# Third and fourth product exchanged in the later blocks of an input phase, with their row factors computed on VectorE

## The chip, the cores and the metric

The kernel runs on one core of a Trainium2 chip. A core has five engines with instruction queues of their own, which the profile names PE (TensorE: matmuls; PEld is its weight load), DVE (VectorE), ACT (ScalarE), POOL (GpSimd) and SP (SyncE, which here only issues DMAs). The queues run side by side and wait for each other by semaphores. Within a queue the instructions of this program run in the order in which they stand.

The metric is the device time of one execution in microseconds (us). The time before is the median of three executions, 921.17 us, with the lowest at 918.97 and the highest at 922.02.

## The reference

With a depth of 1 only the pooling mixer runs: a norm over rows, an input projection into `u` and `gate`, trailing means of `u` over windows of 2, 4, 8 and 16 frames for four groups of 256 channels, a linear map for each group, the product with `silu(gate)`, the output projection, the residual and a final norm. `x` has 4096 rows of 1024 float32 numbers.

```python
def rms_norm(x, w):
    y = xf * lax.rsqrt(jnp.mean(xf * xf, axis=-1, keepdims=True) + RMS_EPS)
    return (y * w.astype(jnp.float32)).astype(x.dtype)

def pool_mixer(h, in_w, group_w, group_b, scale, out_w):
    u, gate = jnp.split(h @ in_w, 2, axis=-1)
    ...
    pooled = jnp.stack([trailing_mean(ug[:, :, g], w) for g, w in enumerate(POOL_WINDOWS)],
                       axis=2) - ug
    mixed = jnp.einsum('bsgc,gcd->bsgd', pooled, group_w) + group_b
    y = mixed.reshape(b, s, POOL_WIDTH) * scale * jax.nn.silu(gate)
    return y @ out_w

h = x + pool_mixer(rms_norm(x, norm_w), ...)
return rms_norm(h, final_norm_w)
```

## The kernel before

**Seven products instead of eight.** Each matrix product is cut into 2 x 2 blocks and done with seven block products, P1 to P7, on sums and differences of the blocks (the Winograd form of Strassen's method). The kernel has 112 such products, which its list of steps (L949 to L951) puts one behind the other: phase "a" (half of the input projection) for four blocks of 1024 rows, phase "b" (the other half) for the same four blocks, and phase "o" (the output projection) for eight blocks of 512 rows. In the phases "a" and "b" the order within a block is `ORDER_IN`, P1, P2, P6, P7, P5, P4, P3. A block of rows has a half 0 ("11" and "12" are its two halves of the channels) and a half 1 ("21" and "22").

**Operands.** TensorE takes each operand as a high and a low part. `split` (L153) makes them: ScalarE copies the operand into the rounded format (the high part, L151), and VectorE subtracts that copy from the operand (the low part, L145). `mm3` (L565) then issues three matmuls for each pair: high with high, high with low, low with high. So the first matmul of a product uses high parts alone, and the second needs a low part. A product in the phases "a" and "b" is 48 matmuls of 128x512 into four of the eight PSUM banks. There are four operand buffers (`ops`), two for each product, so a product's split waits until the product two steps before it has read its buffers.

**Banks.** `bank_of` (L574): P1, P2, P7 and P4 use banks 0 to 3; P6, P5 and P3 use banks 4 to 7. P1 goes through its banks one after the other; the others go through all four with the first half of the depth and then through all four again with the second. `evict_in` (L699) reads the results. ScalarE copies P1's four banks into banks 4 to 7, where P6 and P5 go on adding; P2 is added to P1 in banks 0 to 3, and ScalarE takes the sum through SiLU into two tiles; ScalarE copies P6 into two tiles and P7 into two others; VectorE adds P5 to P7's tiles and P4 to P6's; ScalarE copies P3.

**Forming the operands of phase "a".** P1 takes "11" and P2 takes "12", multiplied by the row factors of half 0 (`normalize`, L454). P6 takes "22" - ("11" - "21") and P7 takes "11" - "21", with "21" and "22" multiplied by the row factors of half 1. `normalize_a2` (L526) does the four multiplications of half 1; it is called as the step of P1 begins (L1211), ahead of P2's split. The four differences (`form_in`, L507, for P6) come right behind it. `form_s4` (L548) takes P6's operand from "12", for P3. P5 takes "11" plus P6's operand. While an operand is split, ScalarE's queue issues a DMA that saves "11", "12", "21" (as P7's operand) and "22" for phase "b" (`split_halves`, L469).

**Row factors.** For block b+1 they are made while block b is multiplied. ScalarE squares and sums rows (`square_row`, L403); `stats` (L412) calls `rsqrt` (L190): ScalarE's square root, VectorE's reciprocal, and one Newton step, which for blocks 1 to 3 is POOL's: `ms` (L193), two products, a multiply-add and a last product (L206 to L211). At the next step `store_rs` (L419) writes the 512 factors to DRAM from POOL's queue, and `load_rstd` (L449) loads them back spread over all partitions, also from POOL's queue. Block 0 goes another way, by matmuls (`spread_rs`).

**Pooling.** `pool` (L617) runs some steps behind the products: VectorE forms the window sums, subtracts and multiplies by the SiLU tile, and SP stores that product to DRAM (`yd`, L685). Its tiles return to a rotation from which later evictions and loads take theirs (`Slots`, `take`); a tile that is taken again must first have been read by whatever used it, a store included.

**What sets the order.** The main loop (L1193 to L1257) walks through the steps. At step n it issues loads up to three steps ahead, the squares and `stats`, the forming of step n + 2 (ahead of the split, unless `normal` holds, L1213: then behind it), the split of step n + 1, due pooling, and the matmuls and evictions of step n. A scheduler then places the instructions on each engine; `tc.issue_after(x)` keeps what stands in it behind instruction x. With block 2 `save_t3` (L273) prepares a difference of weight blocks for phase "b", behind P6: for each of two halves two loads, a subtraction on VectorE and a store. During block 3 the weights of phase "b" are formed and split (`form_wb`, `split_wb`).

**The end.** Behind the last product stand 36 matmuls (L1259 to L1280) that multiply operands still in SBUF with one another in several layouts, into banks that nothing reads afterwards.

Of the kernel before, what the change touches and what calls it, by code (L numbers as in the profile page):

```python
# [15 lines left out]
P = 128  # L16
# [4 lines left out]
NB = S // TB  # L21
# [10 lines left out]
ORDER_IN = (P1, P2, P6, P7, P5, P4, P3)  # L32
ORDER_OUT = (P1, P7, P6, P2, P5, P4, P3)
# [27 lines left out]
def kernel(  # L61
# [128 lines left out]
    def rsqrt(dst, tmp, ms, ss, on_vector=False):  # L190

        root = nc.scalar.activation(tmp, ss, AF.Sqrt, bias=eps, scale=1.0 / D).ins
        nc.gpsimd.tensor_scalar(  # L193
# [218 lines left out]
    def stats(b, half):  # L412
# [3 lines left out]
        rsqrt(rs, tmp, ms, sums[b, half], b == 0)  # L416
# [79 lines left out]

    def load_in(q, b, i):
        s = xs[b]
        if i == P1:
            s["11"] = load_saved(b, P1) if q else load_x(b, 0, 0)  # L500
        elif i == P2:
            s["12"] = load_saved(b, P2) if q else load_x(b, 0, 1)
        elif i == P6:
            s["21"] = load_saved(b, P7) if q else load_x(b, 1, 0)
            s["22"] = load_saved(b, P4) if q else load_x(b, 1, 1)

    def form_in(q, b, i):  # L507

        s = xs[b]
        if i in (P1, P2):  # L510
            if q == 0:
                for u in s["11" if i == P1 else "12"]:
                    normalize(b, 0, u)
        elif i == P6:
            s["2"] = [take() for _ in range(2)]
            for h in range(2):
                if q == 0:
                    sub(s["21"][h], s["11"][h], s["21"][h])
                sub(s["2"][h], s["22"][h], s["21"][h])
        elif i == P5:  # L520
# [4 lines left out]

    def normalize_a2(b):  # L526
        for h in range(2):
            normalize(b, 1, xs[b]["21"][h])
            normalize(b, 1, xs[b]["22"][h])
        give(rstd.pop(b))  # L530

    def split_in(q, b, i):
# [8 lines left out]
        if i not in (P1, P2, P6):  # L541
# [407 lines left out]
    steps = [("a", b, i) for b in range(NB) for i in ORDER_IN]  # L949
# [230 lines left out]
    def row_plan(b):  # L1180
        if b == 0:
# [5 lines left out]
            {P1: (0, 1), P2: (2, 3), P6: (4, 5), P7: (6, 7)},  # L1187
            {P6: (0, 1), P7: (2, 3), P5: (4, 5), P4: (6, 7)},
# [4 lines left out]
    for n in range(2, len(steps)):  # L1193
        kind, b, i = steps[n]
        ahead = kind == "a" and b + 1 < NB
        keep[0] = 5 if kind == "b" and b == NB - 1 else 3
        advance("load", n, load, load_reach)
        if ahead:
# [5 lines left out]
            for j in squares.get(i, ()):  # L1204
                with tc.issue_after(evicted[0]):
                    square_row(b + 1, j // 4, j % 4)
                if j % 4 == 3:
                    scales[j // 4] = stats(b + 1, j // 4)
            for j in rows.get(i, ()):
                load_row(b + 1, j // 4, j % 4, early if b == 0 and i == P6 else None)  # L1210
        if kind == "a" and b > 0 and i == P1:  # L1211
            normalize_a2(b)
        normal = kind == "a" and step(n + 2)[2] in (P1, P2)  # L1213
# [3 lines left out]
        if normal:  # L1217
            with tc.issue_after(latest_split[0]):
                form(n + 2)
        if n == 2:  # L1220
# [37 lines left out]

    sets = sets_of("o", NBO - 1)  # L1259
    left, right = ops[0], w[P1][0]  # L1260
    ways = (
        lambda r: r[:, 0:256].rearrange("p (s a) -> p a s", s=2),
        lambda r: r.rearrange("p (s a) -> p a s", s=2)[:, 0:128],
        lambda r: r[:, 0:256],
        lambda r: r.rearrange("p (m s a) -> p m a s", m=2, s=2),
    )
# [66 lines left out]
```

## Time and profile before

| | us |
|---|---|
| median of three executions | 921.17 |
| lowest and highest | 918.97, 922.02 |
| the profiled execution | 921.6 |
| its span, first to last instruction | 919.8 |
| mean granted TensorE clock | 1.000 of full speed |

The page's second part cuts the span into 40 slices of 23 us. Each digit is the busy share of an engine in tenths.

```profile
PE   9999999999989999999999999999999999999999
PEld 7888888878878888888888888888888888888888
DVE  3898993795697997496686588589988677676675
ACT  6869447347345565346345545654424424324333
POOL 0023101001100000000000000000001001001010
```

Phase "a" fills the slices 3 to 14, phase "b" those to 27, phase "o" the rest. TensorE is at 9 nearly throughout, but a digit of 9 covers a hole of up to 2.3 us. In a line of the timeline stand the start, the duration from the first to the last of the merged instructions, engine, line, operation, output and inputs, form and count, and in brackets how long the engine was idle before and what ended that. A line of the waits gives who waited for whom, the total in us, the number of waits and the longest.

The work of the stages, by windows of the profile (each line: the stretch in us, its length, the busy time of PE, PEld, DVE, ACT and POOL with their instructions, the granted clock, the share and the rate of DMA). The four stretches are about one block of phase "a" each:

```profile
66.00:108.00 42.00, 42.00 (x196) 36.77 (x195) 38.14 (x46) 31.15 (x47) 13.15 (x14) 1.00 0.69 243
108.00:181.00 73.00, 72.22 (x335) 62.93 (x334) 52.66 (x56) 39.22 (x63) 5.18 (x14) 1.00 0.60 204
181.00:256.00 75.00, 73.24 (x340) 63.82 (x339) 55.69 (x59) 39.30 (x64) 5.09 (x14) 1.00 0.64 229
256.00:332.00 76.00, 73.38 (x339) 63.63 (x338) 69.80 (x75) 39.81 (x59) 0.00 (x0) 1.00 0.62 229
```

(The first of them begins inside block 0.)

### The profile page before, as it was taken

How to read it: one execution, taken by the hardware profiler on the slowest of the kernel's cores; microseconds unless marked ns; L12 is line 12 of the kernel's file. 1: busy time of each engine (PE TensorE's matmuls, PEld its weight loads, DVE VectorE, ACT ScalarE, POOL GpSimd, SP SyncE). 2: the span in 40 equal slices, each digit the busy share in tenths (PEclk: the TensorE clock that was granted, in tenths of full speed). 3: DMA queues.
4: the chain of work that ended last, by engine and by line, in shares of the span. 5: the costliest groups of instructions: out<-in, count | busy, mean ns of one | idle time of the engine just before them, and what ended most of it. 6: DMA issues, size and time to landing. Idle time of an engine off the chain costs nothing.

```text
span 919.8 us, 11280 instructions
## 1 busy us (share of the span) xinstructions
PE 910.0 (99%) x4248; PEld 793.3 (86%) x4248; DVE 702.7 (76%) x769; ACT 458.2 (50%) x741; POOL 51.6 (6%) x130
## 2 busy tenths in 40 slices
PE   9999999999989999999999999999999999999999
PEld 7888888878878888888888888888888888888888
DVE  3898993795697997496686588589988677676675
ACT  6869447347345565346345545654424424324333
POOL 0023101001100000000000000000001001001010
DMA  9986666565756626116604725746656446356122
GB/s 342 402 313 212 268 237 202 184 248 205 252 229 238 219 109 216 42 46 229 251 37 134 275 92 195 244 149 203 233 178 230 147 150 229 122 199 210 42 92 92
DMA packets 66518, 177.02 MB, mean 192 GB/s; under 512 B 6048, under 2 KB 23840, under 8 KB 66464
## 3 DMA queue, kind: packets, MB, share of 16 engines
q1 hardware_dynamic: 59888, 154.78, 47.4%
q10 hardware_dynamic: 4176, 13.65, 3.7%
q0 software_dynamic: 2400, 7.88, 2.5%
q8 instruction: 33, 0.54, 0.2%
q14 instruction: 21, 0.17, 0.1%
HBM read 115.45 MB, written 60.83 MB: 192 GB/s over the span
## 4 chain that ended last, share of the span: by engine, by line
PE 79%; DVE 9%; DMA 6%; ACT 4%; issue 2%; SPq 0%; POOL 0%; DVEq 0%; ACTq 0%; POOLq 0%
PE bank L570 78%; DMA early<-in_wut 2%; DVE st L148 2%; DVE op L145 2%; DMA st<-in_x 2%; DMA st<-rd 1%; DMA rd<-rs 1%; DVE vt L142 1%; DVE st L145 1%; ACT op L151 1%; ACT early L407 1%; DVE st L142 1%; ACT st L407 1%; ACT vt L407 1%; PE bank L1275 1%
## 5 line engine op out<-in xcount | busy, mean ns | idle before, releaser
L570 PE MATMUL bank<-op,w 128*128 128x512 f32 x2688 | 582.3, 379 | 6.4 <-DVE op L145 5.7
L570 PEld LDWEIGHTS bank<-op,w 128*128 128x128 f32 x2688 | 507.5, 189 | 80.6 <-DVE op L145 7.8
L570 PE MATMUL bank<-w,op 128*128 128x512 f32 (+1 forms) x1356 | 290.3, 377 | 0.0
L570 PEld LDWEIGHTS bank<-w,op 128*128 128x128 f32 x1356 | 254.6, 189 | 35.8
L151 ACT ACTIVATE op<-st 128x1024 fp32r<-128x1024 f32 x126 | 132.4, 1052 | 167.1 <-PE bank L570 150.3
L145 DVE TENSOR_TENSOR op<-st,op 128x1024 fp32r<-128x1024 f32 x126 | 152.9, 1221 | 69.7 <-ACT op L151 69.4
L151 ACT ACTIVATE op<-vt 128x1024 fp32r<-128x1024 f32 x40 | 42.2, 1056 | 76.4 <-PE bank L570 66.3
L151 ACT ACTIVATE vt<-bank 128x512 f32<-128x512 f32 x102 | 58.5, 593 | 37.0 <-PE bank L570 35.0
L913 DVE TENSOR_TENSOR st<-bank,st 128x512 f32<-128x512 f32 x60 | 41.0, 686 | 29.3 <-PE bank L570 29.1
L145 DVE TENSOR_TENSOR st<-st,st 128x1024 f32<-128x1024 f32 x38 | 46.0, 1222 | 20.6 <-DMA st<-wvd 9.2
L145 DVE TENSOR_TENSOR op<-vt,op 128x1024 fp32r<-128x1024 f32 x40 | 48.8, 1221 | 7.8 <-ACT op L151 7.6
L193 POOL TENSOR_SCALAR oms<-oss 128x2 f32<-128x2 f32 x14 | 9.2, 659 | 607.1 <-ACT st L802 601.0
L151 ACT ACTIVATE bank<-bank 128x512 f32<-128x512 f32 x48 | 27.9, 581 | 26.9 <-PE bank L570 21.5
L142 DVE TENSOR_TENSOR vt<-bank,vt 128x512 f32<-128x512 f32 (+1 forms) x55 | 35.9, 678 | 2.2 <-PE bank L570 2.2
L651 DVE TENSOR_TENSOR_SCAN vt<-vt,bf 128x512 f32<-128x512 f32 x28 | 34.5, 1269 | 0.2 <-ACT vt L151 0.2
L913 DVE TENSOR_TENSOR vt<-bank,vt 128x512 f32<-128x512 f32 (+1 forms) x37 | 24.8, 673 | 12.0 <-PE bank L570 11.7
L145 DVE TENSOR_TENSOR w<-st,w 128x1024 fp32r<-128x1024 f32 x20 | 24.2, 1220 | 12.3 <-ACT w L151 12.3
L673 DVE SCALAR_TENSOR_TENSOR vt<-vt,vt 128x1024 f32<-128x1024 f32 x24 | 29.1, 1214 | 0.0
L148 DVE TENSOR_TENSOR st<-st,st 128x1024 f32<-128x1024 f32 (+1 forms) x19 | 21.7, 1163 | 9.7 <-DMA st<-rd 9.0
L151 ACT ACTIVATE w<-st 128x1024 fp32r<-128x1024 f32 x20 | 20.9, 1055 | 16.2 <-PE bank L570 14.9
L806 DVE SCALAR_TENSOR_TENSOR st<-st,ors,st 128x1024 f32<-128x1024 f32 x17 | 21.4, 1281 | 6.1 <-POOL ors L211 6.1
L151 ACT ACTIVATE vt<-vt 128x1024 f32<-128x1024 f32 (+1 forms) x12 | 11.8, 985 | 25.2 <-DVE vt L142 21.6
(132 smaller groups left out, 570.9 us busy)
## 6 DMA issues: line engine op xcount, KB each, us to landing
st<-in_x SPq DMA_DIRECT2D x33, 512.0 KB, 5.1
st<-sd SPq DMA_DIRECT2D x29, 512.0 KB, 4.8
st<-in_xt SPq DMA_DIRECT2D x25, 512.0 KB, 6.7
vt<-in_x SPq DMA_DIRECT2D x24, 512.0 KB, 4.6
sd<-st ACTq DMA_DIRECT2D x19, 512.0 KB, 4.4
yd<-vt SPq DMA_DIRECT2D x19, 512.0 KB, 2.9
st<-yd SPq DMA_DIRECT2D x19, 512.0 KB, 4.4
out<-st SPq DMA_DIRECT2D x17, 512.0 KB, 4.2
```

The lines of the kernel that those rows point to most:

```text
L142: nc.vector.tensor_tensor(out=dst, in0=a, in1=b, op=ALU.add)
L145: return nc.vector.tensor_tensor(out=dst, in0=a, in1=b, op=ALU.subtract)
L148: nc.vector.tensor_tensor(out=dst, in0=a, in1=b, op=ALU.mult)
L151: return nc.scalar.activation(dst, src, func)
L193: nc.gpsimd.tensor_scalar(out=ms, in0=ss, scalar1=1.0 / D, scalar2=EPS, op0=ALU.mult, op1=ALU.add)
L407: nc.scalar.activation(u[:, 0], u[:, 0], AF.Square, accum_out=sums[b, half][:, j : j + 1])
L570: latest[0] = nc.tensor.matmul(ps, a, b, start=start and n == 0, stop=stop and n == 2, skip_group_check=True).ins
L651: nc.vector.tensor_tensor_scan(s[:, j, at:end], v[:, j, at:end], v[:, j, at - win : end - win], sums_of[j] if sums_of else 0.0, ALU.add, A ...
L673: nc.vector.scalar_tensor_tensor(out=s[:, :, at : at + H], in0=s[:, :, at : at + H], scalar=1.0 / win, in1=v[:, :, HIST:], op0=ALU.mult, o ...
L806: nc.vector.scalar_tensor_tensor(out=us[j], in0=us[j], scalar=rs[:, j : j + 1], in1=fw[0], op0=ALU.mult, op1=ALU.mult,)
L913: partial["added"] = nc.vector.tensor_tensor(out=dst, in0=src, in1=dst, op=ALU.add).ins
L1275: nc.tensor.matmul(ps.rearrange("p (m a s) -> p m a s", m=2, s=2) if c == 3 else ps.rearrange("p (a s) -> p a s", s=2) if c < 2 else ps, l ...
```

## The change

1. In the blocks 1, 2 and 3 of phase "a" the order becomes P1, P2, P7, P6, P5, P4, P3. "21" is loaded for P7 and "22" for P6, a step later than before.
2. `normalize_a2` is gone. For P7 the two multiplications of "21" and the differences "11" - "21" are formed together; for P6 those of "22" and the differences with P7's operand. For P7, P6 and P5 of those blocks forming comes behind the latest split, as it did for P1 and P2.
3. `stats` runs behind the latest split of its step instead of ahead of it, and for the blocks 1 to 3 all of its small operations but the square root are VectorE's. In block 0 `ms` stays on POOL.
4. The plan of the rows that are squared names P7 and P6 in exchanged places, so each row keeps its step.
5. `save_t3` still follows P6 of block 2, which is now the fourth step of the block.
6. The 36 matmuls at the end are left out.

The number of matmuls of the products, of wide operations and of loads and stores is the same.

```diff
--- before.py
+++ after.py
@@ -30,6 +30,7 @@
 
 P1, P2, P3, P4, P5, P6, P7 = range(1, 8)
 ORDER_IN = (P1, P2, P6, P7, P5, P4, P3)
+ORDER_LATER = (P1, P2, P7, P6, P5, P4, P3)
 ORDER_OUT = (P1, P7, P6, P2, P5, P4, P3)
 
 
@@ -190,7 +191,7 @@
     def rsqrt(dst, tmp, ms, ss, on_vector=False):
 
         root = nc.scalar.activation(tmp, ss, AF.Sqrt, bias=eps, scale=1.0 / D).ins
-        nc.gpsimd.tensor_scalar(
+        (nc.vector if on_vector == "all" else nc.gpsimd).tensor_scalar(
             out=ms, in0=ss, scalar1=1.0 / D, scalar2=EPS, op0=ALU.mult, op1=ALU.add
         )
         nc.vector.reciprocal(out=dst, in_=tmp)
@@ -413,7 +414,7 @@
         ms = small.tile([P, 4], F32, tag="ms", name=f"ms{b}_{half}")
         tmp = small.tile([P, 4], F32, tag="tmp", name=f"tmp{b}_{half}")
         rs = small.tile([P, 4], F32, tag="rs", name=f"rs{b}_{half}")
-        rsqrt(rs, tmp, ms, sums[b, half], b == 0)
+        rsqrt(rs, tmp, ms, sums[b, half], "all" if b else "most")
         return rs
 
     def store_rs(b, half, rs):
@@ -494,14 +495,20 @@
             us.append(u)
         return us
 
+    def swapped(q, b):
+        return q == 0 and b > 0
+
     def load_in(q, b, i):
         s = xs[b]
         if i == P1:
             s["11"] = load_saved(b, P1) if q else load_x(b, 0, 0)
         elif i == P2:
             s["12"] = load_saved(b, P2) if q else load_x(b, 0, 1)
+        elif i == P7 and swapped(q, b):
+            s["21"] = load_x(b, 1, 0)
         elif i == P6:
-            s["21"] = load_saved(b, P7) if q else load_x(b, 1, 0)
+            if not swapped(q, b):
+                s["21"] = load_saved(b, P7) if q else load_x(b, 1, 0)
             s["22"] = load_saved(b, P4) if q else load_x(b, 1, 1)
 
     def form_in(q, b, i):
@@ -511,23 +518,24 @@
             if q == 0:
                 for u in s["11" if i == P1 else "12"]:
                     normalize(b, 0, u)
+        elif i == P7 and swapped(q, b):
+            for h in range(2):
+                normalize(b, 1, s["21"][h])
+            for h in range(2):
+                sub(s["21"][h], s["11"][h], s["21"][h])
         elif i == P6:
             s["2"] = [take() for _ in range(2)]
             for h in range(2):
                 if q == 0:
-                    sub(s["21"][h], s["11"][h], s["21"][h])
+                    normalize(b, 1, s["22"][h])
                 sub(s["2"][h], s["22"][h], s["21"][h])
+            if q == 0:
+                give(rstd.pop(b))
         elif i == P5:
             for h in range(2):
                 add(s["11"][h], s["2"][h], s["11"][h])
             for u in s.pop("2"):
                 give(u)
-
-    def normalize_a2(b):
-        for h in range(2):
-            normalize(b, 1, xs[b]["21"][h])
-            normalize(b, 1, xs[b]["22"][h])
-        give(rstd.pop(b))
 
     def split_in(q, b, i):
         s = xs[b]
@@ -538,7 +546,10 @@
             stores.extend(zip(sd[0][i], s[key]))
         if i == P6 and (q or b):
             form_s4(b)
-        if i not in (P1, P2, P6):
+        if i == P6 and swapped(q, b):
+            for u in s.pop("21"):
+                give(u)
+        elif i not in (P1, P2, P6) and not (i == P7 and swapped(q, b)):
             for u in s.pop(key):
                 give(u)
         return t
@@ -946,7 +957,7 @@
 
 
 
-    steps = [("a", b, i) for b in range(NB) for i in ORDER_IN]
+    steps = [("a", b, i) for b in range(NB) for i in (ORDER_LATER if b else ORDER_IN)]
     steps += [("b", b, i) for b in range(NB) for i in ORDER_IN]
     steps += [("o", b, i) for b in range(NBO) for i in ORDER_OUT]
     split_up = {}
@@ -1184,8 +1195,8 @@
                 {P7: range(4), P5: (4, 5), P4: (6, 7)},
             )
         return (
-            {P1: (0, 1), P2: (2, 3), P6: (4, 5), P7: (6, 7)},
-            {P6: (0, 1), P7: (2, 3), P5: (4, 5), P4: (6, 7)},
+            {P1: (0, 1), P2: (2, 3), P7: (4, 5), P6: (6, 7)},
+            {P7: (0, 1), P6: (2, 3), P5: (4, 5), P4: (6, 7)},
         )
 
     scales = {}
@@ -1193,6 +1204,7 @@
     for n in range(2, len(steps)):
         kind, b, i = steps[n]
         ahead = kind == "a" and b + 1 < NB
+        rows_done = None
         keep[0] = 5 if kind == "b" and b == NB - 1 else 3
         advance("load", n, load, load_reach)
         if ahead:
@@ -1205,18 +1217,22 @@
                 with tc.issue_after(evicted[0]):
                     square_row(b + 1, j // 4, j % 4)
                 if j % 4 == 3:
-                    scales[j // 4] = stats(b + 1, j // 4)
+                    rows_done = j // 4
             for j in rows.get(i, ()):
                 load_row(b + 1, j // 4, j % 4, early if b == 0 and i == P6 else None)
-        if kind == "a" and b > 0 and i == P1:
-            normalize_a2(b)
-        normal = kind == "a" and step(n + 2)[2] in (P1, P2)
+        ahead_of = step(n + 2)
+        normal = kind == "a" and ahead_of[2] in (P1, P2) or (
+            ahead_of[0] == "a" and ahead_of[1] > 0 and ahead_of[2] in (P7, P6, P5)
+        )
         if n > 2 and not normal:
             form(n + 2)
         advance("split", n, split_step, split_reach)
         if normal:
             with tc.issue_after(latest_split[0]):
                 form(n + 2)
+        if rows_done is not None:
+            with tc.issue_after(latest_split[0]):
+                scales[rows_done] = stats(b + 1, rows_done)
         if n == 2:
             with tc.issue_after(first_saves[0]):
                 for place, u in stores:
@@ -1256,29 +1272,6 @@
                 )
                 fw.append(f)
 
-    sets = sets_of("o", NBO - 1)
-    left, right = ops[0], w[P1][0]
...
-    with tc.issue_after(latest[0]):
-        for c, way in enumerate(ways):
-            for j in range(9):
...
-                nc.tensor.matmul(
...
```

16 lines of the change are left out of this document (removed).

## The prediction

> **What bounds the kernel now.** I read the page first, then TensorE's waits, its timeline, and the timelines of VectorE and ScalarE around each hole.
>
> ```profile
> PE 910.0 (99%) x4248; PEld 793.3 (86%) x4248; DVE 702.7 (76%) x769; ACT 458.2 (50%) x741; POOL 51.6 (6%) x130
> ...
> L570 PE MATMUL bank<-op,w 128*128 128x512 f32 x2688 | 582.3, 379 | 6.4 <-DVE op L145 5.7
> ```
> ```profile
> PE bank L570 <- DVE op L145: 5.7, 5, 1.9
> ```
> ```profile
> 59.66 59.73 PE L570 MATMUL bank<-op,w 128*128 128x512 f32 x276
> 120.17 10.20 PE L570 MATMUL bank<-op,w 128*128 128x512 f32 x46 [0.79 <-DVE op L145]
> ...
> 194.72 5.45 PE L570 MATMUL bank<-op,w 128*128 128x512 f32 x24 [1.76 <-DVE op L145]
> ...
> 257.90 10.63 PE L570 MATMUL bank<-op,w 128*128 128x512 f32 x48 [0.75 <-DVE op L145]
> 270.39 4.80 PE L570 MATMUL bank<-op,w 128*128 128x512 f32 x21 [1.86 <-DVE op L145]
> ...
> 349.71 272.98 PE L570 MATMUL bank<-op,w 128*128 128x512 f32 x1264
> ```
>
> TensorE is the bound: it is idle for 1% of the span. What an edit of the input phase can win is therefore the sum of its holes. There are five waits of matmuls on the operand split (5.7 us); the timeline places four of them (0.79, 1.76, 0.75, 1.86) and shows no hole from 59.66 to 119.4, so the fifth, about 0.5 us, lies before, in block 0, whose order stays. Uninterrupted matmuls start 272.98/1264 = 0.216 us apart while each is drawn 0.379 us long, so a hole costs 0.163 us more than its idle time: 5.16 + 4 x 0.163 = **5.81 us**. A product has 48 matmuls, 10.4 us, and a block of seven takes 72.6 us; so the holes are block 1 P2, block 2 P2, and block 3 P1 and P2.
>
> VectorE's timeline shows why, in block 2 (first fence) and in blocks 3 and 1 (second and third).
>
> ```profile
> 172.50 1.23 DVE L148 TENSOR_TENSOR st<-st,st 128x1024 f32<-128x1024 f32 x1 [3.94 <-DMA st<-rd]
> ...
> 180.96 2.35 DVE L145 TENSOR_TENSOR op<-st,op 128x1024 fp32r<-128x1024 f32 x2
> 183.23 2.35 DVE L148 TENSOR_TENSOR st<-st,st 128x1024 f32<-128x1024 f32 x2
> 185.50 1.22 DVE L148 TENSOR_TENSOR vt<-vt,st 128x1024 f32<-128x1024 f32 x1
> 186.63 1.22 DVE L148 TENSOR_TENSOR st<-st,st 128x1024 f32<-128x1024 f32 x1
> 187.77 1.22 DVE L148 TENSOR_TENSOR vt<-vt,st 128x1024 f32<-128x1024 f32 x1
> 188.90 2.36 DVE L145 TENSOR_TENSOR st<-st,st 128x1024 f32<-128x1024 f32 x2
> 191.18 2.36 DVE L145 TENSOR_TENSOR st<-vt,st 128x1024 f32<-128x1024 f32 x2
> 193.45 2.36 DVE L145 TENSOR_TENSOR op<-st,op 128x1024 fp32r<-128x1024 f32 x2
> ```
> ```profile
> 248.18 1.23 DVE L148 TENSOR_TENSOR st<-st,st 128x1024 f32<-128x1024 f32 x1 [5.07 <-DMA st<-rd]
> ...
> 256.63 2.35 DVE L145 TENSOR_TENSOR op<-st,op 128x1024 fp32r<-128x1024 f32 x2
> ...
> 269.12 2.35 DVE L145 TENSOR_TENSOR op<-st,op 128x1024 fp32r<-128x1024 f32 x2
> ```
> ```profile
> 107.54 6.90 DVE L148 TENSOR_TENSOR st<-st,vt 128x1024 f32<-128x1024 f32 x6
> ```
>
> P2's first split (193.45) ends at 194.67, and the second matmul of P2, the first that needs a low half, starts at 194.72. Between P1's splits and P2's stand the two normalizations for P2 (183.23), three of the second half's and the four differences; the fourth normalization was put far ahead, at 172.50, and held all of VectorE 3.94 us (5.07 in block 3) until its row factors had come back from DRAM.
>
> **The change part by part.** (1) *Normalizations and differences behind P2's split.* In the order in which the changed program's instructions stand on VectorE, P2's splits follow P2's two normalizations directly. Seven operations leave that place in blocks 2 and 3 and eight in block 1 (four of the six at 107.54 and four differences), one every 2.36 - 1.22 = 1.14 us: 7 x 1.14 = 8.0 us. P2's first split of block 2 would end at 186.7 instead of 194.7; TensorE asked for it at 194.72 - 1.76 = 192.96, and will ask 0.95 us earlier once block 1's hole is gone. The second split is held by its operand buffer, which P3 of the block before reads to its end; a copy (1.06 us by ScalarE's rows below) and a split (1.22) later is still some 8 us before P2. So P2's holes (0.79, 1.76, 1.86) go.
>
> (2) *The normalization that held VectorE.* In the new order none of the second half's stands ahead of P2's splits. For P1 of block 3 that is 5.07 + 1.14 = 6.2 us; the first split would start at 250.4. TensorE will have gained 2.9 us by then (0.79 + 1.76 + 2 x 0.163), and stopped at 257.15 in the old count, so it asks at 254.3. Split, plus the small operations of (3), ends at about 252.5: nearly 2 us to spare. This hole goes too.
>
> (3) *Row factors on VectorE.* Six times five 128x4 operations leave POOL and five more stand on VectorE.
>
> ```profile
> 43.77 0.18 DVE L196 RECIPROCAL rs<-tmp 128x4 f32<-128x4 f32 x1 [1.55 <-ACT tmp L192]
> 44.06 0.16 DVE L148 TENSOR_TENSOR tmp<-rs,ms 128x4 f32<-128x4 f32 x1
> ```
> ```profile
> 235.22 0.20 POOL L206 TENSOR_TENSOR tmp<-rs,ms 128x4 f32<-128x4 f32 x1 [3.36 <-DVE rs L196]
> ...
> 236.07 0.20 POOL L211 TENSOR_TENSOR rs<-rs,tmp 128x4 f32<-128x4 f32 x1
> ```
> ```profile
> 236.68 4.65 DMA rd<-rs
> ...
> 241.73 6.42 DMA st<-rd
> ```
>
> Five of at most 0.18 us are 0.9 us per set, 5.4 in all, on an engine 76% busy; behind idle slots they are free, and the bound if all six hit TensorE is 5.4. I take 0, nearer the spare times of (1) and (2). More weighs that they now stand behind P3's split and between the next pooling work: counting that order at 1.14 us a wide operation, the second half's factors are ready some 9 us later than 236.3. Their way out and back took 236.27 to 248.15, 11.9 us; they then land near 256 (2.9 us taken off), and P7's normalizations, their first user, stand behind P2's second split, which ends near 258. From there two normalizations, two differences, the pooling of P3 and two splits take about 14 us, to 272; P7 begins at 254.3 + 20.7 = 275.0. So the factors have some 5 us of slack.
>
> (4) *P6.* Its normalizations, differences and the differences of P3's operand come a product later, with P7's whole product as cover. The T3 preparation (two loads each way on SP's queue) also moves a step, behind P6; P1's inputs of block 3 reuse its tiles.
>
> ```profile
> st<-in_xt SPq DMA_DIRECT2D x25, 512.0 KB, 6.7
> ```
>
> The T3 tiles come free with P5's splits of block 2, near 217; behind these, two loads and two stores in turn, at 4.5 us or less each (rival B's last row), and one input load, 4 x 4.5 + 6.7 = 24.7 us, end near 242, for splits near 250. P5 now follows P6 in the same banks, with the slack worked out in rival B. I take 0; the upper end is B's.
>
> (5) *The 36 trailing matmuls.*
>
> ```profile
> SPq L1329 <- DMA out<-vt: 1.9, 3, 0.8
> ```
> ```profile
> 912.69 5.19 PE L1275 MATMUL bank<-w,op 128*128 128x256 f32 x36
> ```
> ```profile
> 917.50:918.00 0.50, 0.38 (x2) 0.00 (x0) 0.00 (x0) 0.00 (x0) 0.00 (x0) 1.00 0.92 336
> 918.00:918.50 0.50, 0.00 (x0) 0.00 (x0) 0.00 (x0) 0.00 (x0) 0.00 (x0) 1.00 0.06 16
> ```
>
> They end at 917.9; output packets still move at 918.0 and SP waits for those landings last. The chain names the matmuls only because semaphore steps are no work. Removing them gains 0, at most 0.1.
>
> **Sum**, against the profiled execution's 921.6 us (span 919.8, 1.8 around it): 921.6 - 5.8 = 915.8. That execution is 0.4 above the median of 921.17, so I predict **915.4 us**, -0.63%.
>
> **Rivals.** *B: P7 waits for P2's banks.* P7 starts the very four banks that P2 has just filled; before, P6 lay between. A bank is complete 18 matmuls (3.9 us) before the next product returns to it, and its eviction takes 0.60 us, so ScalarE may be 3.3 us late. But it can be:
>
> ```profile
> 201.29 0.60 ACT L151 ACTIVATE vt<-bank 128x512 f32<-128x512 f32 x1 [0.24 <-PE bank L570]
> ...
> 205.17 1.06 ACT L151 ACTIVATE op<-st 128x1024 fp32r<-128x1024 f32 x1 [1.99 <-PE bank L570]
> 209.88 1.09 ACT L151 ACTIVATE st<-bank 128x512 f32<-128x512 f32 x2 [3.65 <-DVE st L142]
> ```
> ```profile
> 133.68 1.09 ACT L151 ACTIVATE st<-bank 128x512 f32<-128x512 f32 x2 [2.00 <-DMA yd<-st]
> ```
> ```profile
> DMA to landing us min/median/max: 2.9/3.7/4.5
> ```
>
> The first two fences are ScalarE in blocks 2 and 1, the last the two stores of pooled products near 200 to 210. The third and fourth evictions of P2 write a tile whose pooled product must first land in DRAM. P2 of block 2 ended at 194.72 + 47 x 0.216 = 204.9; bank 2 was clear at 210.5, and P7 would have wanted it 12 matmuls in, at 207.5: 3.0 us lost. In block 1 the same count gives 1.2. Left as late, the loss is 1.2 + 3.0, and 919.6 results. Against it: in the new order three wide operations fewer (3.4 us) stand between P1's splits and that product's last multiply, and the held VectorE (5.1 in block 2) is gone; that moves the store some 5 us forward against P2's end, 2 us better than needed. The Trainium skill, "PSUM — Partial Sum Buffer", section "PSUM bank collisions raise a hardware error", says to guard PSUM by whole bank; by it no matmul of P7 could slip in beside an eviction, and the price is the 4.2 us above. No row of the trace before shows such a wait.
>
> *C: VectorE stays late in block 3.* Its weight preparations start there; if P1's and P2's holes stay (0.75 + 1.86 + 0.33 = 2.9 us), 918.3. For it: less than 2 us spare at P1. Against it: the 8.0 us of (1).
>
> *D, slower: the factors come back too late.* Place: P7's two normalizations, at the head of VectorE's queue, in each of the three blocks; behind them wait the pooling and P7's splits, and TensorE for these. It decides from the slack of 5 us, a way out and back of 17 us; beyond it each us costs one per block. At 20 us: 3 x 3 = 9 us, 924.4. Against it: 11.9 in the quoted row. The Trainium skill, "SBUF — State Buffer", section "SBUF: two separate sides", warns that DMAs issued by GpSimd wait for their descriptors while VectorE holds the shared port; by that a wait of one wide operation at each of the two DMAs adds 2.4 us at most, inside the slack. No run so far separates that wait from the 11.9.
>
> *E: it doesn't do what it says*, the normalization being hoisted again: the changed order excludes it, so it gets no chance of its own.
>
> **How the numbers follow.** The forecast 0.64 (913.7 to 917.2 with the spread of the three runs, 918.97 to 922.02), B 0.18 (from one us lost, 916.4, to 919.6), C 0.10, D 0.08. 0.3%, about what a measurement of this kernel tells from no change, is 2.8 us: faster means below 918.4. The forecast, half of B and half of C give 0.78 faster, 0.14 same, D 0.08 slower. The range reaches to B's far end and leaves out D and the scatter beyond: 913.5 to 919.7.
>
> **What would show it.** (1), (2): TensorE's waits on the split fall to about 0.5 us, in block 0 alone; if holes of 0.7 to 1.9 us remain after 100 us, I am wrong there. (3): the five small operations on VectorE at 0.1 to 0.2 us, no POOL arithmetic from 70 to 260 us, P7's normalizations not waiting on the factor load by more than 5 us. (4), B: no wait of TensorE on ScalarE's evictions; if there is one, it stands 12 or 18 matmuls into P7. (5): the last output landing some 6 us behind the last product, as now. A product rate other than 0.216 us would overturn all of it.

## The result, and the profile after

The changed kernel takes 917.35 us in the median of seven runs (916.17 to 918.14), the kernel before 922.02 in seven runs beside it (918.97 to 923.11): ratio **0.9955**, 95% interval 0.9940 to 0.9969. The profiled execution took 917.93 us with a span of 916.2 (919.8 before). The medians differ by 4.7 us, the two profiled spans by 3.7; what follows accounts for the spans.

TensorE's waits, from the page and the waits of the kernel after:

```profile
PE 904.7 (99%) x4212; PEld 788.9 (86%) x4212; DVE 706.4 (77%) x799; ACT 457.1 (50%) x741; POOL 34.8 (4%) x100
...
L581 PE MATMUL bank<-op,w 128*128 128x512 f32 x2688 | 582.1, 379 | 2.7 <-DVE op L146 1.9
```
```profile
PE bank L581 <- DVE op L146: 1.9, 2, 1.3
```

The products' matmuls waited 6.4 us before and 2.7 now, and for the operand split 1.9 us in two waits instead of 5.7 in five. One of the two waits is in block 0, as before. TensorE's timeline (start, duration of the merged matmuls, count, idle time before and what ended it) over the later blocks of phase "a":

```profile
99.72 156.37 PE L581 MATMUL bank<-op,w 128*128 128x512 f32 x722
257.38 42.86 PE L581 MATMUL bank<-op,w 128*128 128x512 f32 x196 [1.29 <-DVE op L146]
```

The holes at P2 of all three blocks are gone. One of 1.29 us is new, at 257.38: P1 of block 3, but at its eighth matmul and not at its second. VectorE's timeline ahead of it:

```profile
234.05 1.23 DVE L146 TENSOR_TENSOR st<-st,st 128x1024 f32<-128x1024 f32 x1 [5.65 <-DMA st<-wvd]
...
242.69 1.23 DVE L149 TENSOR_TENSOR st<-st,vt 128x1024 f32<-128x1024 f32 x1 [2.74 <-DMA st<-in_xt]
243.83 0.16 DVE L194 TENSOR_SCALAR ms<-ss 128x4 f32<-128x4 f32 x1
243.90 0.17 DVE L197 RECIPROCAL rs<-tmp 128x4 f32<-128x4 f32 x1
...
249.33 0.15 DVE L204 TENSOR_TENSOR rs<-rs,tmp 128x4 f32<-128x4 f32 x1
...
252.33 1.21 DVE L146 TENSOR_TENSOR op<-st,op 128x1024 fp32r<-128x1024 f32 x1
253.46 2.73 DVE L692 SCALAR_TENSOR_TENSOR st<-vt,colt,st 128x512 f32<-128x512 f32 x4
256.11 1.22 DVE L146 TENSOR_TENSOR op<-st,op 128x1024 fp32r<-128x1024 f32 x1
```

VectorE waited for a load of the T3 preparation (5.65 us) and then for P1's input (2.74). P1's first split came in time, at 252.33. Its second stands behind four multiplications of the pooling, ends at 257.33, and the eighth matmul starts at 257.38.

To add up, I take from the trace every pair of successive matmuls of the products that start more than 0.3 us apart, block 0 left out, and count what exceeds the usual 0.216 us. So counted, a hole holds the 0.163 us that the prediction added, and each is followed by a further 0.10 at the next matmul. Before, the holes come to 6.23 us (5.82 and four times 0.10). After, there are three: 1.46 at P1 of block 3, and 0.27 and 0.19 at the thirteenth matmul of P7 of blocks 1 and 3; with the tenths 2.23. Block 1 also starts 0.35 us later (109.00 for 108.65), which is block 0's. 6.23 - 2.23 - 0.35 = 3.65, and the spans differ by 3.67. The whole difference of these two profiles lies in these holes.

### The profile page after: what moved, and what is told of

Read it like the earlier page. It is cut to its first block, busy times and chain, and to the rows that moved or that the text cites. A ratio compares the mean times of both kernels' runs of the same rounds, so it can differ in the third digit from the quotient of the medians.

```text
span 916.2 us, 11193 instructions
## 1 busy us (share of the span) xinstructions
PE 904.7 (99%) x4212; PEld 788.9 (86%) x4212; DVE 706.4 (77%) x799; ACT 457.1 (50%) x741; POOL 34.8 (4%) x100
## 4 chain that ended last, share of the span: by engine, by line
PE 82%; DVE 7%; ACT 4%; DMA 4%; issue 2%; DVEq 0%; ACTq 0%; SPq 0%
PE bank L581 80%; PE bank L374 3%; DVE op L146 1%; DMA st<-wvd 1%; DVE st L149 1%; ACT early L408 1%; DMA st<-in_xt 1%; ACT op L152 1%; DVE vt L143 1%; DMA st<-in_x 1%; DVE st L146 1%; DVE st L143 1%; DVE st L692 1%; DVE vt L146 0%; DMA yd<-st 0%
## 5 line engine op out<-in xcount | busy, mean ns | idle before, releaser
L146 DVE TENSOR_TENSOR st<-st,st 128x1024 f32<-128x1024 f32 x35 | 42.5, 1221 | 18.9 <-DMA st<-sd 7.8
L143 DVE TENSOR_TENSOR vt<-bank,vt 128x512 f32<-128x512 f32 (+1 forms) x51 | 33.2, 679 | 1.6 <-PE bank L581 1.6
L924 DVE TENSOR_TENSOR vt<-bank,vt 128x512 f32<-128x512 f32 (+1 forms) x37 | 24.8, 673 | 11.7 <-PE bank L581 11.4
L149 DVE TENSOR_TENSOR st<-st,vt 128x1024 f32<-128x1024 f32 x23 | 27.2, 1218 | 2.7 <-DMA st<-in_xt 2.7
L152 ACT ACTIVATE st<-bank 128x512 f32<-128x512 f32 x30 | 17.5, 595 | 23.5 <-PE bank L581 10.5
```

The source lines that it names most:

```text
L143: nc.vector.tensor_tensor(out=dst, in0=a, in1=b, op=ALU.add)
L146: return nc.vector.tensor_tensor(out=dst, in0=a, in1=b, op=ALU.subtract)
L149: nc.vector.tensor_tensor(out=dst, in0=a, in1=b, op=ALU.mult)
L152: return nc.scalar.activation(dst, src, func)
L924: partial["added"] = nc.vector.tensor_tensor(out=dst, in0=src, in1=dst, op=ALU.add).ins
```

## The experiments

Each is compared with the kernel before on its own chip. "Holes" are those of its profile, counted as above, without the tenths; in the sum they are included.

| run | ratio (95% interval) | holes | sum |
|---|---|---|---|
| before | | block 1 P2 0.95, block 2 P2 1.93, block 3 P1 0.92, P2 2.03 | 6.23 |
| after | 0.9955 (0.9940 to 0.9969) | block 3 P1 1.46, P7 0.19, block 1 P7 0.27 | 2.23 |
| without the 36 matmuls | 1.0007 (0.9993 to 1.0022) | block 1 P2 0.96, block 2 P2 1.69, block 3 P2 2.02 | 4.99 |
| factors alone | 0.9950 (0.9938 to 0.9962) | block 1 P2 1.08 | 1.18 |
| order alone | 0.9945 (0.9933 to 0.9958) | block 3 P1 1.11, P7 0.18 | 1.50 |
| all eight behind P2's split | 0.9950 (0.9938 to 0.9963) | block 3 P6 1.32, phase "b" P6 0.79 | 2.31 |
| after, again | 0.9951 (0.9939 to 0.9964) | block 3 P1 0.30, P7 0.18, block 1 P7 0.20 | 0.99 |
| after, T3 earlier | 0.9940 (0.9927 to 0.9952) | block 1 P7 0.61 | 0.71 |
| after, 36 matmuls back | 0.9950 (0.9937 to 0.9963) | block 3 P1 0.10, P7 0.19 | 0.39 |
| after, T3 earlier, pooling ahead | 0.9942 (0.9928 to 0.9956) | block 2 P5 0.42 | 0.53 |
| one multiplication back in its place | 0.9954 (0.9940 to 0.9967) | block 1 P2 0.74 | 0.85 |
| block 1's eight behind | 1.0000 (0.9989 to 1.0010) | block 2 P1 0.42, P2 2.03, block 3 P1 0.90, P2 2.03 | 5.79, and 1.61 at a lower clock |
| both of these | 0.9939 (0.9925 to 0.9952) | none | 0 |
| after, T3 earlier, again | 0.9940 (0.9927 to 0.9952) | block 1 P7 0.24 | 0.34 |

### The parts one by one

**The 36 matmuls left out of the kernel before.** Nothing reads what they compute.

```diff
-    with tc.issue_after(latest[0]):
-        for c, way in enumerate(ways):
...
-                nc.tensor.matmul(
...
```

> The kernel before without its 36 trailing matmuls, which write banks that nothing reads. Theory (they end before the last output lands): the same time as before within 0.6 us, ratio 1.000. Rival (the chain of waits puts 5.0 us on them, so they hold the end): 4 to 5 us faster, ratio 0.995.

Measured: 1.0007, an interval that holds 1. From the start of the last product's last matmul to the end of the span it is 7.2 us with them (912.58 to 919.82) and without them in the kernel after (908.92 to 916.15). No cost shows. Nor does one in the kernel after, with the 36 matmuls back: 916.80 us beside 917.02 (further down).

This run also repeats the kernel before with another landing: in block 3 the early multiplication waited 4.11 us for its factors instead of 5.07, and P1's hole of 0.92 us is not there.

**The factors alone**, in the kernel before: `stats` behind the latest split, its small operations on VectorE.

```diff
...
-                    scales[j // 4] = stats(b + 1, j // 4)
+                    rows_done = j // 4
...
+        if rows_done is not None:
+            with tc.issue_after(latest_split[0]):
+                scales[rows_done] = stats(b + 1, rows_done)
```

> The kernel before with part 3 of the change alone: row factors on VectorE, behind the latest split; products, normalizations and differences in the old order. Theory (the gain comes from the normalizations that leave the place ahead of P2's split): no gain, ratio 1.000 +- 0.002; P1's hole of block 3 (0.91 us) closes as the hoisted normalization is gone, but the second half's factors come some 9 us later and P2's splits wait behind them, so P2's holes stay or grow, in blocks 1 and 3 to 2 or 3 us. Rival (the row factors bring the gain): ratio 0.995, P2's holes gone.

Measured: 0.9950. The theory, that this part is worth nothing, is wrong, and so is the forecast that P2's holes stay or grow. TensorE's and VectorE's timelines of this run:

```profile
99.77 20.02 PE L570 MATMUL bank<-op,w 128*128 128x512 f32 x92
120.70 219.56 PE L570 MATMUL bank<-op,w 128*128 128x512 f32 x1016 [0.92 <-DVE op L145]
```
```profile
177.88 1.22 DVE L145 TENSOR_TENSOR op<-st,op 128x1024 fp32r<-128x1024 f32 x1
179.01 3.49 DVE L148 TENSOR_TENSOR st<-st,st 128x1024 f32<-128x1024 f32 x3
182.42 1.22 DVE L148 TENSOR_TENSOR vt<-vt,st 128x1024 f32<-128x1024 f32 x1
183.56 1.22 DVE L148 TENSOR_TENSOR st<-st,st 128x1024 f32<-128x1024 f32 x1
184.69 1.22 DVE L148 TENSOR_TENSOR vt<-vt,st 128x1024 f32<-128x1024 f32 x1
185.83 2.36 DVE L145 TENSOR_TENSOR st<-st,st 128x1024 f32<-128x1024 f32 x2
188.10 2.36 DVE L145 TENSOR_TENSOR st<-vt,st 128x1024 f32<-128x1024 f32 x2
190.37 2.36 DVE L145 TENSOR_TENSOR op<-st,op 128x1024 fp32r<-128x1024 f32 x2
```

From block 2 on TensorE has no hole left; block 1's (1.08 us) stays. Yet between P1's second split (177.88) and P2's splits (190.37) stand P2's two multiplications and all eight operations of the second half, one more than before. What is missing is the multiplication that stood at 172.50 and waited 3.94 us: it has moved back to the other three.

**The order alone**, in the kernel after: `stats` and its POOL operations as before.

```diff
-        rsqrt(rs, tmp, ms, sums[b, half], "all" if b else "most")
+        rsqrt(rs, tmp, ms, sums[b, half], b == 0)
...
+                    scales[j // 4] = stats(b + 1, j // 4)
...
```

> The changed kernel with the row factors as before the change: Newton step on POOL, ahead of the split. Theory: the whole gain stays, ratio 0.995, no hole at P2 in blocks 1 to 3; the hole of 1.45 us inside P1 of block 3 stays or shrinks by no more than the small operations' 0.5 us. Rival (the small operations on VectorE make P1 of block 3 late): that hole is gone, 1.4 us less than the changed kernel. Rival (the row factors bring the gain): ratio 1.000.

Measured: 0.9945. P2's holes are gone, and a hole of P1 in block 3 is there as in the kernel after.

**The kernel before with the four multiplications and four differences behind P2's splits**, P6 still third.

```diff
-        if kind == "a" and b > 0 and i == P1:
-            normalize_a2(b)
-        normal = kind == "a" and step(n + 2)[2] in (P1, P2)
+        second = kind == "a" and b > 0 and i == P1
+        normal = kind == "a" and step(n + 2)[2] in (P1, P2) or second
...
+                if second:
+                    normalize_a2(b)
```

> The kernel before, with the four normalizations of the second half and P6's four differences put behind P2's split, and nothing else: P6 stays third and P7 fourth. Theory (what counts is the place of these eight operations): P2's holes (0.94, 1.92, 2.02) and P1's of block 3 (0.91) go; in block 3 a new hole of 0 to 2 us appears ahead of P6, whose eight operations, pooling and splits (16 to 17 us of VectorE behind P2's splits) have only P2's product and P1's rest as cover; ratio 0.994 to 0.997. Rival (the exchange itself is needed): the holes move whole to P6 in all three blocks, ratio 0.999 to 1.002.

Measured: 0.9950. The exchange isn't needed for the gain. The holes at P2 and P1 are gone. The price shows in block 3, where the pooling now stands between the differences and P6's first split (TensorE's timeline, then VectorE's):

```profile
276.10 64.15 PE L570 MATMUL bank<-op,w 128*128 128x512 f32 x296 [1.15 <-DVE op L145]
```
```profile
268.95 1.22 DVE L145 TENSOR_TENSOR st<-vt,vt 128x1024 f32<-128x1024 f32 x1
270.09 1.22 DVE L145 TENSOR_TENSOR vt<-vt 128x1024 f32<-128x1024 f32 x1
...
274.82 1.22 DVE L145 TENSOR_TENSOR op<-st,op 128x1024 fp32r<-128x1024 f32 x1
```

A second new hole, 0.79 us at P6 in phase "b", was not followed up.

So each of three edits alone gives the whole gain within the intervals: they overlap. Common to all three is that no multiplication of the second half is placed ahead of P1's splits any more. Two of them also move the eight operations behind P2's splits, as the prediction's step (1) counted it.

### One instruction

**The kernel before with `normalize_a2` kept behind P1's latest split**; the source has no other edit:

```diff
         if kind == "a" and b > 0 and i == P1:
-            normalize_a2(b)
+            with tc.issue_after(latest_split[0]):
+                normalize_a2(b)
```

> The kernel before with one edit: the four multiplications of the second half are kept behind P1's latest operand split, so that none can be placed ahead of P1's splits. On VectorE exactly one operation moves in block 2 and one in block 3 (the multiplication that waited 3.94 and 5.07 us for its row factors now stands with the other three); block 1 is unchanged, all eight operations still stand ahead of P2's splits in every block, the factors stay on POOL, P6 stays third. Theory (the early multiplication and its wait make blocks 2 and 3 late): the holes at P2 of block 2 (1.93), P1 (0.92) and P2 (2.03) of block 3 go, only block 1's (about 1.0) stays; 6.2 less 1.1 is 5 us, ratio about 0.995 (0.9935 to 0.997). Rival (the eight operations' place ahead of P2's splits, as the prediction's step 1 has it): P2 of blocks 2 and 3 stays held, the first split some 8 us later than it could be; only P1's hole of block 3 goes, and ratio is 0.999 to 1.000.

Measured: 0.9954. TensorE's timeline, and VectorE's around P2 of block 2:

```profile
99.69 20.23 PE L570 MATMUL bank<-op,w 128*128 128x512 f32 x93
120.51 179.84 PE L570 MATMUL bank<-op,w 128*128 128x512 f32 x832 [0.58 <-DVE op L145]
```
```profile
173.48 1.21 DVE L145 TENSOR_TENSOR op<-st,op 128x1024 fp32r<-128x1024 f32 x1
...
177.26 1.22 DVE L145 TENSOR_TENSOR op<-st,op 128x1024 fp32r<-128x1024 f32 x1
178.40 3.48 DVE L148 TENSOR_TENSOR st<-st,st 128x1024 f32<-128x1024 f32 x3
...
189.75 2.35 DVE L145 TENSOR_TENSOR op<-st,op 128x1024 fp32r<-128x1024 f32 x2
```

The theory holds and the rival falls: with eight operations ahead of P2's splits, the first split ends at 190.97 instead of 194.67. That is 3.70 us earlier, nearly the 3.94 that the multiplication had waited, and early enough for P2, whose second matmul starts at 192.92. Holding back **one VectorE instruction in block 2 and one in block 3** removes three of the four holes; 6.23 - 0.85, less 0.54 by which block 1 starts later here (109.19), is 4.84 us, and the spans differ by 4.8 (919.8 and 915.0).

The expectation that nothing else moves was not met: the scheduler now places P1's first split four half multiplications of the pooling earlier (173.48; before, 180.96, directly ahead of the second split), and likewise in block 3. For P2's holes this makes no difference, since the same work stands ahead of P2's splits in either order. For P1's hole of block 3 it isn't needed: there even P1's second split, behind that pooling, is over at 251.0, and P1's second matmul starts at 255.08.

**Only block 1's eight operations behind P2's splits**, blocks 2 and 3 as before:

```diff
-        if kind == "a" and b > 0 and i == P1:
+        second = kind == "a" and b == 1 and i == P1
+        if kind == "a" and b > 1 and i == P1:
             normalize_a2(b)
...
+                if second:
+                    normalize_a2(b)
```

> The kernel before with the four multiplications and four differences of block 1 alone placed behind P2's splits; blocks 2 and 3 are as before, the early multiplication with its wait among them. Theory (in block 1, where no multiplication is placed early, the eight operations' place makes the hole; in blocks 2 and 3 it is the early wait): block 1's hole (0.95) goes, the holes of blocks 2 and 3 stay, about 5 us together or up to 1 us more where the wait is set by a landing that doesn't move; ratio 0.9988 to 1.0005. Rival (block 1's lateness is what the later blocks inherit): all holes go, ratio 0.995.

Measured: 1.0000. Block 1's hole went, so there the place of the eight operations makes it. Of the 1.05 us (the hole and its tenth) 0.62 came back in this profile: TensorE reaches block 2 earlier, VectorE does not, a hole of 0.42 opens at P1 of block 2, which had none, and P2's grows from 1.93 to 2.03. The 0.4 us that are left are too few for the interval to show. VectorE's timeline shows the wait that sets the new hole:

```profile
172.23 1.23 DVE L148 TENSOR_TENSOR st<-st,st 128x1024 f32<-128x1024 f32 x1 [4.56 <-DMA st<-rd]
```

In this profile 1.6 us more were lost in block 3 to a lower granted clock (last section). Such losses show in the kernel before as well, so this one is not put down to the edit.

**Both edits together.**

> The kernel before with the edits of the last two runs together: the multiplications of the second half behind P1's splits in blocks 2 and 3, and behind P2's splits, with the four differences, in block 1. P6 stays third, the factors stay on POOL, the 36 matmuls at the end stay. Theory: with the early multiplication gone (0.85 us of holes left, all in block 1) and block 1's eight operations out of the way, no hole later than block 0 is left; span 0.7 to 0.9 us below that of the run with the first edit alone, ratio 0.9935 to 0.9955. Rival (the holes only move on): a new hole of 0.5 to 1.3 us at P6 of block 1, as the run with all eight behind P2's splits showed at P6 of block 3, and the ratio of the first edit alone.

Measured: 915.75 us, 0.9939 (0.9925 to 0.9952), the lowest median of all runs. TensorE's timeline from 100 to 300 us is one line:

```profile
99.77 200.46 PE L570 MATMUL bank<-op,w 128*128 128x512 f32 x928
```

No hole is left, and the span of the profiled execution is 913.6, 6.2 us below before: all of the 6.23. It keeps the product order, POOL's factors and the 36 matmuls.

### What remained in the kernel after

Four kernels: the kernel after once more, with T3's preparation at the third product of block 2, with the 36 matmuls back, and with the earlier T3 and due pooling ahead of the forming of P7.

```diff
-        if kind == "a" and b == 2 and i == P6:
+        if kind == "a" and b == 2 and i == P7:
             save_t3()
```
```diff
+        if kind == "a" and b > 0 and i == P1:
+            pool_due(n)
```

> The changed kernel once more, as the measure for the other runs beside it: ratio 0.9955 +- 0.0015; holes of 0.2 to 0.4 us at the 13th matmul of P7 in blocks 1 and 3, of 1.45 us at the 8th of P1 in block 3.

> The changed kernel with the T3 preparation a product earlier, behind P7 of block 2, the third step as before the change. Theory (P1's inputs of block 3 reuse tiles of the T3 preparation and come late): the hole of 1.45 us inside P1 of block 3 is gone and nothing else changes, 1.2 to 1.6 us less than the changed kernel. Rival (the small operations and the pooling on VectorE make P1's second split late): the hole stays above 1 us, the time is that of the changed kernel.

> The changed kernel with the 36 trailing matmuls put back. Theory (they end before the last output lands): the time of the changed kernel within 0.6 us, and the mean granted clock back at 1.000, since only the idle end was counted at half clock. Rival (they held the end): 1 to 5 us more.

> As y2, and in the later blocks the pooling that is due at P1 comes ahead of P7's normalizations. Theory (P7's 13th matmul waits for a bank whose eviction waits for a pooled product's store): that store is issued some 4.5 us earlier, the holes in P7 of blocks 1 and 3 (0.27 and 0.18 us) go too; 1.6 to 2.0 us less than the changed kernel. Rival (P7's splits, now later, are waited for): a hole at the first matmuls of P7, no gain over y2.

Measured: 0.9951, 0.9940, 0.9950, 0.9942. With T3 earlier VectorE no longer waits for P1's input of block 3:

```profile
236.27 2.35 DVE L149 TENSOR_TENSOR st<-st,vt 128x1024 f32<-128x1024 f32 x2
...
249.69 1.22 DVE L146 TENSOR_TENSOR op<-st,op 128x1024 fp32r<-128x1024 f32 x1
```

P1's multiplications start at 236.27 instead of 242.69, its second split at 249.69 instead of 256.11, and the hole is gone. The difference of about 1 us (917.02 to 916.05) lies within overlapping intervals; the trace shows where it would come from. With the late T3 the hole goes with the time at which VectorE gets P1's first input: 1.46, 1.11, 0.30 and 0.10 us with 242.69, 242.63, 241.49 and 241.26 in four profiles (after, order alone, after again, 36 matmuls back). The 1.46 of the first profile is the largest of them: the kernel after, run again, lost 0.30 there, where its expectation said 1.45. The 36 matmuls changed nothing measurable. Nor did the pooling, for which a gain was expected: P7's holes went, and one of 0.42 us came at P5 of block 2, where TensorE waits for an eviction.

> The changed kernel with the preparation of the T3 tiles a step earlier, once more, on the same chip as the kernel before with both small edits. Theory: both have almost no hole left, so the two agree within 0.1% (ratio 0.994 for each). Rival: the exchange with its waits of P7 for P2's banks (0.61 and 0.27 us so far) keeps this kernel 0.5 to 1 us behind.

Measured: 915.95 us (0.9940) beside 915.75 (0.9939) for the two small edits on the same chip: the same, as the theory said.

## Why the prediction was right, and where it was wrong

The number was near: 915.4 with 913.5 to 919.7, against 917.35, and -0.63% against -0.45%. Some of that is luck: 917.35 lies just above the forecast's own band (913.7 to 917.2) and is covered because the range was drawn out to rival B's far end, while B gave only 0.46 us. The sum was too large by the holes that remained. By the prediction's own sign, a hole of 0.7 to 1.9 us past 100 us, it was wrong at P1 of block 3 (1.46). And the number hides that for the larger part the prediction saw half of the cause.

- **What bounds the kernel: right.** The spans differ by what the holes differ by, in the kernel after and in the two small edits, alone and together (for block 1's eight with the 1.6 us of the lower clock).
- **Step (1), half of the cause.** It gave P2's holes in all three blocks to the eight operations ahead of P2's splits. For block 1 that is shown (0.95 us). In blocks 2 and 3 (1.93 and 2.03) the same operations in the same place leave no hole once the multiplication ahead no longer waits. Whether moving them alone, with the wait kept, would have been enough there is not shown; by the step's own count, 8.0 us against a hole of 2, it would. So in the kernel after these holes go twice over. The step asked what stands between P1's splits and P2's, and not why P1's splits were late already. It let P2's first split of block 2 end at 186.7 by taking seven operations away, while the wait of step (2) and its multiplication come off too, 3.94 + 1.14 more; the kernel after has that split at 180.50, ending at 181.73 (194.67 - 8.0 - 5.08 = 181.6).

```profile
180.50 1.23 DVE L146 TENSOR_TENSOR op<-st,op 128x1024 fp32r<-128x1024 f32 x1
```

- **Step (2), mechanism right, credit too small and one split forgotten.** The early multiplication's wait was given one hole (P1 of block 3); without it three go, 4.87 of the four holes' 5.82 us. The step also says: "Split, plus the small operations of (3), ends at about 252.5: nearly 2 us to spare." That was the first split, which only started at 252.33; P1's eighth matmul needs the second, which stood behind four half multiplications and ended at 257.33. 1.46 us were lost there. With T3 earlier the second split stands behind the same four and costs nothing, so it took step (4)'s delay as well.
- **Step (3), right in result.** The thirty small operations added take 0.15 to 0.17 us in the quoted rows, and VectorE's whole busy time rose by 3.7 (706.4 - 702.7), which TensorE never saw. The factors of block 3 were ready at 249.48, 13 us later than 236.27 and not 9, because VectorE had stood still twice (with T3 earlier they are ready at 243.06); no wait of VectorE on the factor load is left (9.0 us in two waits before). The way out was shorter than assumed: from the store's issue to the load's, 2.1 us (249.88 to 251.96) for 5.1. No run shows the two waits of a wide operation that the prediction's rival D adds there. That this part alone gives 0.5% I had not foreseen: I costed where its operations land and not what else moves when the factors come later.
- **Step (4), half right.** P1's inputs were forecast to land near 242; VectorE got the first at 242.69. The splits were forecast near 250 and started at 252.33 and 256.11. "I take 0" was wrong, and this is the term of the sum that failed: with the first multiplication at 242.69, everything behind it in VectorE's queue, the pooling and the second split, came late, 1.46 us for TensorE in this profile and 0.30 in the kernel's second. T3 a product earlier removes it.
- **Step (5), right:** 0.
- **Rival B came, at a tenth of its size**: 0.27 us in block 1 for 1.2, none in block 2 for 3.0, and 0.19 in block 3, which it had not counted. ScalarE's timeline of the kernel after shows the mechanism as argued in block 1, an eviction held until a pooled product has landed:

```profile
131.93 1.09 ACT L152 ACTIVATE st<-bank 128x512 f32<-128x512 f32 x2 [4.00 <-DMA yd<-st]
...
278.82 0.60 ACT L152 ACTIVATE st<-bank 128x512 f32<-128x512 f32 x1 [3.92 <-DVE st L149]
```

  The first of the two copies is over near 132.5, and P7's thirteenth matmul, the first that returns to that bank, starts at 132.58. In block 3 the eviction waited for a multiplication on VectorE instead, was over at 279.42, and the matmul starts at 279.47. The Trainium skill, "PSUM — Partial Sum Buffer", section "PSUM bank collisions raise a hardware error", says to guard by bank; the trace agrees, with waits of 0.27 and 0.19 us at that matmul.
- **Rival C came in part:** not the old holes, but VectorE late in block 3. **D did not:** P7's first normalization of block 3 ran at 263.13 with no wait.

What stays open: why the multiplication was placed early in the kernel before. The scheduler places it there when nothing holds it back, and does not when the factors come later; by what rule was not tried.

## What to carry to other kernels

When an engine's in-order queue shows an idle stretch that ends with a transfer's landing, first look whether the instruction that waited could have stood later; hold it behind what TensorE needs next, and measure that alone before reordering anything larger. Holes downstream of such a wait can be its, as three were here, even where other work stands directly ahead of the late instruction. When several parts of a change each remove the same wait, trying them one by one shows it: their gains don't add.

## What the runs showed of the hardware

POOL's small operations on 128x4 elements take 0.20 us or five times that, at different places of the kernel before (POOL's timeline, then VectorE's):

```profile
76.56 0.20 POOL L206 TENSOR_TENSOR tmp<-rs,ms 128x4 f32<-128x4 f32 x1 [0.19 <-DVE rs L196]
76.83 1.25 POOL L207 TENSOR_TENSOR tmp<-tmp,rs 128x4 f32<-128x4 f32 x1
78.17 1.04 POOL L208 TENSOR_SCALAR tmp<-tmp 128x4 f32<-128x4 f32 x1
79.29 1.06 POOL L211 TENSOR_TENSOR rs<-rs,tmp 128x4 f32<-128x4 f32 x1
```
```profile
76.80 1.23 DVE L145 TENSOR_TENSOR op<-st,op 128x1024 fp32r<-128x1024 f32 x1 [0.39 <-ACT op L151]
77.94 2.36 DVE L145 TENSOR_TENSOR w<-vt,w 128x1024 fp32r<-128x1024 f32 x2
```

The same three took 0.20 us each near 236 us. The Trainium skill, "SBUF — State Buffer", section "SBUF: two separate sides", states that GpSimd and VectorE share a pair of ports that one of them holds for a whole instruction. The trace agrees: each of the three longer ones ends 0.05 to 0.06 us after the operation that VectorE was running when it began (78.08 after 78.02, 79.21 after 79.16, 80.35 after 80.30). Of the 32 small operations of the row factors in the kernel before, ten are long. All ten begin beside a VectorE operation that reads two tiles in SBUF and end 0.05 to 0.06 us after such an operation. The other 22 begin beside none or beside one that reads a bank, but for one at 20.40, in the last 0.13 us of such an operation. No run was made to test it by an edit.

The granted clock can fall to half while the matmuls follow one another without a hole. In the profile of the run with block 1's eight behind, windows of block 3 (length, busy times of PE, PEld, DVE, ACT and POOL, granted clock, DMA):

```profile
272.00:273.00 1.00, 1.00 (x4) 0.82 (x3) 1.00 (x2) 0.00 (x0) 0.00 (x0) 0.50 0.33 123
...
274.00:276.00 2.00, 2.00 (x9) 1.73 (x8) 2.00 (x4) 0.00 (x0) 0.00 (x0) 0.86 0.79 290
```

Seven matmuls in a row start 0.43 us apart there, where the usual distance is 0.216. It began some 1.0 us behind P2's hole of 2.03, lasted some 3.4 us and cost 1.6. The kernel before has the same hole in its profile and a clock of 1.000, so the hole alone is not shown to be the cause.

Of the 50 executions of the kernel before that stand beside the experiments, 13 have a mean clock of 0.998; their median is 922.45 us, that of the 37 at 1.000 is 920.94. Of the 25 executions of the five kernels that keep the 36 matmuls and lost most of the holes, one has 0.998. So part of what a changed kernel gains in the medians can be this clock rather than the holes themselves. With one multiplication back in its place, that kernel and the kernel before beside it ran at 1.000 throughout, and the ratio is 0.9954.

The kernel after has a mean clock of 0.998 for another reason, which costs nothing: its last window, where TensorE has no work left.

```profile
912.00:916.20 4.20, 0.00 (x0) 0.00 (x0) 0.41 (x2) 0.26 (x1) 0.00 (x0) 0.58 0.42 154
```
